# Behind the last product of a streaming encoder layer: 3840 further matmuls of 272 columns

## The chip, the cores and the metric

The kernel runs on one core of a Trainium2 chip. Such a core has a matmul engine (TensorE; PE in the profile, and PEld for its weight loads), a vector engine (VectorE, DVE), a scalar engine (ScalarE, ACT), a general engine (GpSimd, POOL) and an engine that mostly issues transfers (SyncE, SP). A matmul reads a stationary operand, up to 128x128 numbers that a weight load puts into the array, and a moving operand, of which up to 512 columns stream past it; both lie in the on-chip memory SBUF, and the result goes to PSUM, which has eight banks of 512 columns of 32 bits. The metric is the device time of one execution in microseconds (us).

## The reference

One layer of an encoder trunk, for 1024 frames of a new stream and 64 frames of a running one (1088 in all), with a model width of 1024:

```python
def trunk(x, ...):
    m, cs, nk, nv = mixer(rmsnorm(x, g_mix[l]), ...)   # gated convolution and band attention, merged by gates
    x = x + m
    x = x + swiglu(rmsnorm(x, g_ffn[l]), w_ff1[l], w_ff3[l], w_ff2[l])
    return rmsnorm(x, g_final), ...

def swiglu(x, w1, w3, w2):
    return (jax.nn.silu(x @ w1) * (x @ w3)) @ w2
```

The hidden width of the last part is 2816. Outputs are the two normalised results (`y_prompt`, `y_sample`) and the new states of the convolution and the attention. Everything is in float32.

## The kernel before, in words

Each large product is done with split operands. A number is split into a high part, rounded to the type that TensorE takes (`F32R`), and a low part, the rest; a product then is high x high + high x low + low x high, three matmuls that add into one PSUM bank. Above the splitting, large products are cut into 2x2 blocks and done with the seven products of Strassen's scheme, in the order 1, 2, 6, 7, 5, 4, 3 (`STEPS`).

The loop that does this for the input projection and the up and gate products is `run`. For each of the seven products and each of four slices of the depth it issues six matmuls of 272 columns (`HN`): high weights with the high part of the activations, high weights with the low part, low weights with the high part, each for two halves `j` of the frames, which go to two banks. The weights are the stationary operand, and the two halves follow each other with the same weights:

```python
for k in range(4):
    for n, (w, l) in enumerate(((hi, 0), (hi, 1), (lo, 0))):
        for j in range(2):
            mm(t[:, j, :HN], w[:, k, :], x[p][:, l, k, j * HN : (j + 1) * HN], ...)   # L238
```

Other products of 272 columns are plain ones (`product`, L300 to L302): the same three matmuls, one after the other into a single bank.

The last stage is the down product of the feed-forward part (L1508). Its moving operands, 512 columns of the split weights `w_ff2`, lie in rings, one long tile of 4352 numbers per partition for each of the seven products; `ring_of(p)` gives the ring of product `p`. Its stationary operands are tiles `ht` of the hidden activations, read back from `h_d` through SP's queue. The results go to PSUM tiles A (two buffers) and B or D (four buffers in common) of the pool `psD`; ScalarE or VectorE adds them to the accumulators in SBUF (L1518, L1520), and at the end `half_ended` forms the sums of squares (L1448; ScalarE writes the squares, unread, to columns 3072 to 3583 of the first ring), the factor of the normalisation and the output, which leaves by SP's queue (L1459) and ScalarE's (L1457).

The order of the work on each engine is the order in which the program issues it. Tile pools put in the waits that buffers and data need. The program ends with a barrier of all engines (L1587): SP first waits for the counts of all transfers and of the other engines, TensorE's among the last ones.

Of the kernel before, what the change touches and what calls it, by code (L numbers as in the profile page):

```python
# [8 lines left out]
F32 = mybir.dt.float32  # L9
# [6 lines left out]
P = 128  # L16
# [17 lines left out]
HN = HT // 2  # L34
# [30 lines left out]
def encoder_kernel(ctx: ExitStack, tc: tile.TileContext, ins, outs):  # L65
# [1396 lines left out]
    for b, ks in enumerate(blocks):  # L1462
        first, final = b == 0, b == len(blocks) - 1
        nk = blocks[b + 1] if not final else []
        for g in range(2):
# [28 lines left out]
            for si, js in turns:  # L1494
# [47 lines left out]
                if final and g == 0 and si == 4:  # L1542
# [9 lines left out]
                    vec.scalar_tensor_tensor(row, row, r[:TS], gfb[:TS], op0=ALU.mult, op1=ALU.mult)  # L1552
                    nc.sync.dma_start(outs["y_sample"], row)

_OUTS = [
    ("y_prompt", (1024, 1024), (1, 1024, 1024)),
    ("y_sample", (64, 1024), (1, 64, 1024)),
# [33 lines left out]
```

## Time and profile before

| | |
|---|---|
| Median of 2 runs | 1516.43 us (1516.06 to 1516.81) |
| Span of the profiled execution, first to last instruction | 1513.8 us |
| Its own time, with what lies around the span | not in the page; the median is 2.6 us above the span |
| Matmuls, with as many weight loads | 10,178 |
| TensorE busy | 1476.9 us, 98% of the span |
| VectorE, ScalarE, GpSimd busy | 981.2, 682.7, 128.7 us |
| Moved by DMA | 264.73 MB, mean 175 GB/s |
| Mean granted clock of TensorE | 0.994 |

The profile is of one execution. A row that starts with a line number (L238) tells of that line of the kernel; "Da<-mg,wha" means that the tile Da was written from the tiles mg and wha, moving operand first for a matmul; "x4" counts instructions. "128*128" ahead of the shapes is the stationary operand. In the timeline a row begins with its start and its length in us. In the table of stretches each engine has its busy time in us and, in brackets, its instructions in that stretch. Matmuls overlap each other, so that the length of one is longer than the time from its start to the start of the next. SPq and ACTq are the queues on which SP and ScalarE issue transfers, PEq is TensorE's own queue of instructions.

### The profile page before, as it was taken

What the parts mean: (1) busy time and instruction counts of PE and PEld (TensorE: products, weight loads), DVE (VectorE), ACT (ScalarE), POOL (GpSimd) and SP (SyncE); (2) the same over time, 40 slices, a digit from 0 to 9 for tenths busy, and PEclk for the clock granted to TensorE, in tenths of its full rate; (3) what the DMA queues carried; (4) which work ended last, traced back from release to release, by engine and by line L of the source; (5) the groups of instructions that cost most, each with busy time, mean ns of one, the idle gap of its engine ahead of it and who ended that gap; (6) DMA issues with size and microseconds to landing.
All of it is one profiled execution on the core that took longest, in us unless ns stands there. A gap on an engine that the chain in (4) does not pass through costs nothing.

```text
span 1513.8 us, 26451 instructions
## 1 busy us (share of the span) xinstructions
PE 1476.9 (98%) x10178; PEld 1381.1 (91%) x10178; DVE 981.2 (65%) x1843; ACT 682.7 (45%) x1397; POOL 128.7 (9%) x236
## 2 busy tenths in 40 slices
PE   7999999999999999999999999999999999999997
PEld 5799999999999999998889999999999998788886
DVE  6886465642776752763489667666666668857576
ACT  6654433333776752542256444444444445402123
POOL 1210010001111121000100011100001011000000
PEclk9999999999999999999999999999999999999999
DMA  7597524168676529554432434443334449667675
GB/s 233 181 305 245 184 78 135 57 187 234 181 186 176 151 82 293 164 167 145 140 126 77 143 134 152 144 148 120 117 142 157 143 177 317 234 221 235 222 259 202
DMA packets 167518, 264.73 MB, mean 175 GB/s; under 512 B 19008, under 2 KB 103168, under 8 KB 167264
## 3 DMA queue, kind: packets, MB, share of 16 engines
q1 hardware_dynamic: 146736, 198.23, 42.2%
q0 software_dynamic: 19504, 62.71, 11.4%
q10 hardware_dynamic: 1152, 2.10, 0.4%
q8 instruction: 80, 1.31, 0.4%
q14 instruction: 46, 0.38, 0.1%
HBM read 171.06 MB, written 91.92 MB: 174 GB/s over the span
## 4 chain that ended last, share of the span: by engine, by line
PE 79%; DMA 8%; DVE 6%; ACT 3%; issue 3%; SPq 1%; POOL 0%; ACTq 0%; POOLq 0%; DVEq 0%
PE Aa L238 9%; PE Ab L238 9%; PE A L1508 7%; PE Da L238 4%; PE Db L238 4%; PE D L1508 3%; PE Bb L238 2%; PE Ba L238 2%; PE B L1508 2%; PE wo L1066 2%; PE wo L1068 2%; PE wo L1067 2%; PE t L903 2%; PE Ak L238 2%; PE g L300 2%
## 5 line engine op out<-in xcount | busy, mean ns | idle before, releaser
L1508 PE MATMUL A<-ring,ht 128*128 128x512 f32 x528 | 126.6, 393 | 3.6 <-ACT acc L1518 1.9
L1508 PEld LDWEIGHTS A<-ring,ht 128*128 128x128 f32 x528 | 98.8, 188 | 27.2 <-ACT acc L1518 3.2
L300 PE MATMUL g<-xn,whp 128*128 128x272 f32 x384 | 113.2, 295 | 0.0
L301 PE MATMUL g<-xn,whp 128*128 128x272 f32 x384 | 112.0, 292 | 0.0
L302 PE MATMUL g<-xn,wlp 128*128 128x272 f32 x384 | 111.6, 291 | 0.0
L121 ACT CAST ring<-w2r 128x512 fp32r<-128x512 f32 (+1 forms) x78 | 43.4, 587 | 105.7 <-PE A L1508 52.6
L121 ACT CAST hq<-sa 128x512 fp32r<-128x512 f32 x77 | 47.7, 619 | 86.4 <-DVE sa L1239 56.6
L814 DVE CUSTOM_DVE_ANT_0 p<-s,bb 128x640 f32<-128x640 f32 (+5 forms) x72 | 47.5, 661 | 45.5 <-DMA bb<-bias_d 28.6
L1227 POOL DMA_DIRECT2D h_d<-hq x77 | 40.9, 532 | 416.5 <-DVE hq L122 242.1
L122 DVE TENSOR_TENSOR hq<-sa,hq 128x512 fp32r<-128x512 f32 x77 | 53.1, 690 | 33.4 <-ACT hq L121 33.3
L300 PEld LDWEIGHTS g<-xn,whp 128*128 128x128 f32 x384 | 72.6, 189 | 1.0
L302 PEld LDWEIGHTS g<-xn,wlp 128*128 128x128 f32 x384 | 72.6, 189 | 0.5
L301 PEld LDWEIGHTS g<-xn,whp 128*128 128x128 f32 x384 | 72.7, 189 | 0.3
L1508 PE MATMUL D<-ring,ht 128*128 128x512 f32 x264 | 63.9, 393 | 1.3 <-ACT acc L1518 1.3
L122 DVE TENSOR_TENSOR wla<-rawa,wha 128x512 fp32r<-128x512 f32 x56 | 38.5, 687 | 40.5 <-ACT wha L121 40.5
L238 PE MATMUL Aa<-tt,wha 128*128 128x272 f32 x352 | 59.1, 289 | 2.5 <-ACT tt L121 2.5
L1508 PEld LDWEIGHTS D<-ring,ht 128*128 128x128 f32 x264 | 49.5, 188 | 13.1 <-ACT acc L1518 1.8
L122 DVE TENSOR_TENSOR ring<-w2r,ring 128x512 fp32r<-128x512 f32 (+1 forms) x78 | 49.0, 647 | 14.4 <-ACT ring L121 14.2
L238 PE MATMUL Ab<-mg,whb 128*128 128x272 f32 x352 | 58.4, 288 | 0.0
L238 PE MATMUL Aa<-mg,wha 128*128 128x272 f32 x352 | 58.3, 288 | 0.0
L238 PE MATMUL Ab<-tt,whb 128*128 128x272 f32 x352 | 58.2, 287 | 0.0
L121 ACT CAST wha<-rawa 128x512 fp32r<-128x512 f32 x56 | 34.8, 621 | 51.3 <-PE Ab L238 35.3
(519 smaller groups left out, 4368.2 us busy)
## 6 DMA issues: line engine op xcount, KB each, us to landing
h_d<-hq POOLq DMA_DIRECT2D x77, 512.0 KB, 3.5
ht<-h_d SPq DMA_DIRECT2D x154, 256.0 KB, 3.7
rawa<-in_w_ff SPq DMA_DIRECT2D x11, 1024.0 KB, 5.9
rawb<-in_w_ff SPq DMA_DIRECT2D x11, 1024.0 KB, 5.4
w2r<-in_w_ff SPq DMA_DIRECT2D x11, 1024.0 KB, 5.8
qd<-q_d SPq DMA_DIRECT2D x32, 272.0 KB, 4.7
rawp<-in_w_in SPq DMA_DIRECT2D x6, 1024.0 KB, 5.9
u_d<-scr SPq DMA_DIRECT2D x8, 544.0 KB, 4.6
```

What stands on the lines that cost most here:

```text
L121: act.copy(hi, src)
L122: vec.tensor_tensor(lo, src, hi.bitcast(F32), op=ALU.subtract)
L238: mm(t[:, j, :HN], w[:, k, :], x[p][:, l, k, j * HN : (j + 1) * HN], start=p in (1, 2, 7) and k == 0 and n == 0, stop=k == 3 and n == 2, s ...
L300: mm(out, a, p, start=k == 0, stop=False)
L301: mm(out, a, q, start=False, stop=False)
L302: mm(out, b, p, start=False, stop=k == kt - 1)
L814: vec.tensor_tensor_reduce(out=s if len(ps.shape) == 2 else s.rearrange("p (a b) -> p a b", a=2), in0=ps, in1=bias if len(ps.shape) == 2 e ...
L903: nc.tensor.transpose(tp[:, i * P : (i + 1) * P], s[:, i * P : (i + 1) * P], ident)
L1066: mm(ps, x(k, 0), wh, start=f, stop=False)
L1067: mm(ps, x(k, 0), wl, start=False, stop=False)
L1227: nc.gpsimd.dma_start(h_d[p, c - 1], hq.rearrange("p i l t -> p (i l t)").bitcast(F32))
L1508: mm(t, ht[k][:, j, x], w[:, l], start=p in (1, 2, 7) and k == 0 and n == 0, stop=k == len(ks) - 1 and n == 2, skip_group_check=p in (6, 5 ...
```

## The change

Behind the loop of the last stage, 3840 matmuls are added. They write two new PSUM tiles, `pr` and `pq`, that nothing reads. The moving operand is a slice of 272 columns of the first ring, the stationary one a slice of 128 columns of the second ring; both rings hold the split weights of the last block at that point. `a` and `b` are the first columns of the two slices. A setting is a pair of a gap `e` and a shift `d`: `d` moves the stationary operand, by 0 to 120 numbers of 4 bytes in steps of 8, and `e` widens the distance between the two halves of the moving operand, 384 numbers, by 0 to 56 in steps of 8. Each setting is done for four places `k` of the stationary operand, 512 numbers apart, with six matmuls each. In the first 128 settings (`JOINT`) the two halves alternate, in the last 32 (`APART`) all three products of one half come first.

```diff
+    pr = psD.tile([P, 512], F32, tag="A", name="pr", bufs=2)
+    pq = psD.tile([P, 512], F32, tag="BD", name="pq", bufs=4)
+    mv, st = ring_of(1), ring_of(2)
+    JOINT = [(0, 0, 0), (0, 0, 1), (0, 1, 0), (0, 1, 1), (1, 0, 0), (1, 0, 1)]
+    APART = [(w, l, j) for j in range(2) for w, l in ((0, 0), (0, 1), (1, 0))]
+    for six, gaps, starts in ((JOINT, range(0, 64, 8), range(0, 128, 8)), (APART, (0, 16), range(0, 128, 8))):
+        for e in gaps:
+            for d in starts:
+                for k in range(4):
+                    for n, (w, l, j) in enumerate(six):
+                        a, b = 128 + 2048 * l + j * (384 + e), 128 + d + 512 * k + 256 * w
+                        mm(
+                            (pr, pq)[j][:, :HN], st[:, b : b + P], mv[:, a : a + HN],
+                            start=k == 0 and n < 6 and (w, l) == (0, 0), stop=k == 3, skip_group_check=True,
+                        )
```

The outputs are computed as before.

## The prediction

> **What bounds the kernel now.** First the page's head and its row of the granted clock: who is busy, and at what clock.
>
> ```profile
> span 1513.8 us, 26451 instructions
> PE 1476.9 (98%) x10178; PEld 1381.1 (91%) x10178; DVE 981.2 (65%) x1843; ACT 682.7 (45%) x1397; POOL 128.7 (9%) x236
> PEclk9999999999999999999999999999999999999999
> ```
>
> TensorE is busy for 98% of the span, at 9 tenths or more of its clock in every slice. Each of its 10,178 matmuls has a weight load of its own (PEld, same count), also where neighbours share the stationary operand. The time between the starts of two matmuls is therefore a property of the pair, load and matmul. The durations of single matmuls don't give it, because matmuls overlap. It has to come from counts in stretches, or from start times.
>
> The second view is the table of busy times in chosen stretches. The two below hold almost nothing but matmuls of 272 columns: the first is the Strassen loop (L238), whose order the change copies, the second the plain products (L300 to L302), in which all matmuls of a group write one bank.
>
> ```profile
> core 0: us, PE busy (x) PEld busy (x) DVE busy (x) ACT busy (x) POOL busy (x), PEclk, DMA share, GB/s
> 850.00:1150.00 300.00, 300.00 (x2404) 299.94 (x2403) 201.61 (x338) 133.09 (x251) 31.08 (x59) 1.00 0.40 144
> 558.89:598.25 39.36, 39.36 (x315) 39.36 (x314) 6.93 (x9) 11.38 (x25) 6.21 (x12) 1.00 0.85 267
> ```
>
> The counts take in matmuls that began before the window. One lasts 288 ns (rows below), so two or three at a time are in flight, and I take off 2.3. Then the first stretch has 300/2401.7 = **124.9 ns** per matmul, the second 39.36/312.7 = 125.9 ns. The first ran beside a VectorE that was busy two thirds of the time, the second beside one busy 18%, and the quieter one is not the faster. The clock is 1.00 in both.
>
> The timeline shows the same from start to start. The first two rows give one round of six matmuls (four with the high half of the weights, two with the low half), the others its durations and loads:
>
> ```profile
> 901.54 0.66 PE L238 MATMUL Da<-mg,wha 128*128 128x272 f32 x4
> 902.03 0.41 PE L238 MATMUL Da<-mg,wla 128*128 128x272 f32 x2
> ...
> 904.54 0.66 PE L238 MATMUL Aa<-mg,wha 128*128 128x272 f32 x4
> L238 PEld LDWEIGHTS Aa<-mg,wha x352: 187/188/191, 796.0 to 1242.9; 128*128 128x128 f32 x176
> L238 PE MATMUL Aa<-mg,wha x352: 283/288/292, 796.2 to 1243.0; 128*128 128x272 f32 x176
> ```
>
> From 901.54 to 904.54 are four rounds: 24 matmuls in 3.00 us, 125.0 ns each. A load takes 188 ns and a matmul 288 ns, and both come every 125 ns, so they overlap each other.
>
> The third view is the timeline at the end of the span.
>
> ```profile
> 1501.60 2.21 PE L1508 MATMUL D<-ring,ht 128*128 128x512 f32 x9
> 1499.92 0.67 DVE L1520 TENSOR_TENSOR acc<-A,acc 128x512 f32<-128x512 f32 x1
> 1501.80 0.69 DVE L1520 TENSOR_TENSOR acc<-A,acc 128x512 f32<-128x512 f32 x1
> 1503.64 2.20 PE L1508 MATMUL A<-ring,ht 128*128 128x512 f32 x9
> 1505.98 0.68 DVE L1520 TENSOR_TENSOR acc<-A,acc 128x512 f32<-128x512 f32 x1
> 1509.76 0.37 ACTq L1457 DMA_DIRECT2D out_y_prompt<-acc  x1
> out_y_prompt<-acc ACTq DMA_DIRECT2D x4, 256.0 KB, 2.6
> SPq L1587 <- PEq L1587: 0.7, 2, 0.5
> ```
>
> TensorE's last matmul ends at 1503.64 + 2.20 = 1505.84. Behind it come the last additions and the normalisation, and the last output, issued at 1509.76 and landing about 2.6 us later, at 1512.4. The span ends at 1513.8. So TensorE idles 8.0 us at the end, and 1.4 us pass between the last landing and the end, 0.7 us of them SP's waits for TensorE in the closing barrier.
>
> **The change, part by part.** *Removed or moved:* nothing. The orders of VectorE, ScalarE, GpSimd and SP stay as they are, no DMA is added, and the new matmuls stand behind TensorE's last product.
>
> *Their start.* The two new result tiles take banks that the last stage used. pr takes the older of the two "A" banks, last read by the L1520 addition at 1499.92, over at 1500.59. pq takes the bank of the first B product of that stage, read earlier still. So I cost the waits at nothing: the cover is the nine matmuls from 1503.64. If the bank were the younger one, the addition at 1505.98 would hold pr until 1506.66, that is 1 us. The stretch of the first ring tile that ScalarE still writes as scratch (columns 3072 to 3583) is not read: the furthest column read is 128 + 2048 + 440 + 272 = 2888. The nine D matmuls start every (1503.64 - 1501.60)/9 = 0.227 us, so the first new matmul starts at 1503.64 + 9 x 0.227 = **1505.68**.
>
> *Their pace.* 128 + 32 settings of 24 matmuls are 3840. The first 3072 stand in exactly the order of L238: two halves of the columns in turn, in two banks, high weights with the high and the low half of the activations, then low weights. The last 768 do all three products of one half and then those of the other, nearest to L300 to L302, whose three products follow each other in one bank. What no row shows is the particular places: a stationary operand moved in steps of 32 bytes against the moving one, with a fixed relation inside a setting. The matmuls of 512 columns (L1508) show how much places can do in this kernel, since their groups differ only in the tiles' places:
>
> ```profile
> 1480.83 4.24 PE L1508 MATMUL B<-ring,ht 128*128 128x512 f32 x18
> 1484.91 4.36 PE L1508 MATMUL A<-ring,ht 128*128 128x512 f32 x18
> 1489.11 4.36 PE L1508 MATMUL D<-ring,ht 128*128 128x512 f32 x18
> ```
>
> B takes (1484.91 - 1480.83)/18 = 226.7 ns, A (1489.11 - 1484.91)/18 = 233.3 ns: 2.9% between places. By columns, B's rate would make 272 columns 226.7 x 272/512 = 120.4 ns, the **low bound**. The **high bound** for a mean is 124.9 x 1.029 = 128.5 ns, places that lie as far above this kernel's mean as A lies above B. The offsets of the 160 settings run evenly through 512 bytes of relative place, so good and bad ones should average; I take 124.9, the mean of the 300 us in the same order.
>
> *Their sum.* 3839 gaps x 0.1249 = 479.5 us, last start 1985.2. The last matmul adds 0.29: 1985.5. The close lies between the 0.7 of the barrier rows and the 1.4 of the whole stretch; SP has then long passed the output waits and stands at TensorE's count near the end of its list, so I take 1.0. Span after: **1986.5**. The page gives the span of the profiled execution and no time around it; the shown median, 1516.43, lies 2.6 above 1513.8, and I add that: 1989.1.
>
> *What is hidden.* The old tail (8.0 us) now runs beside the new matmuls, so of the 480 us of new work about 472 lengthen the run. Were it not covered (output landing behind the new work), 7 us would come on top.
>
> *A rule that speaks against the sum.* In the rows a matmul of 272 columns takes 124.9 ns in a stream, and one of 512 takes 226.7 to 233.3. The Trainium skill, "TensorE: Matmul & The Clock Gate", section "Back-to-back issue gap", gives for the isolated gap, warm, columns/2.4 + 2.5 ns, an estimate of 115.8 ns at 272 columns, and about 131 ns at 512 columns in a stream of loads and matmuls. By the first figure the sum would be 1954, an estimate from that page; the second disagrees with this trace, which shows 226.7 at least. The same page says (Part 2) that loading the next weights takes no read bandwidth from the running matmul, and so that places could not matter; the 2.9% between A and B doesn't settle it, for the two differ in more than one place.
>
> **The rivals.**
>
> *Free places.* Inside a setting the relative place of the two operands is fixed, where L238 shifts it from matmul to matmul. If most settings then run like B, the pace is 120.4 ns: 1505.68 + 462.2 + 0.29 + 1.0 + 2.6 = **1971.8**. For it: B's rate is steady over 18 matmuls. Against: B is one of three groups, and 850 to 1150 mixes many places at one rate. The page's 115.8 ns would be this rival at its limit; no stretch here ran at it, so I put it at 1 in 50 by itself.
>
> *Colliding places.* Some settings hold load and stream on each other all the time. At 128.5 ns the time is 1505.68 + 493.3 + 3.9 = **2002.9**. The far end is a load that no longer overlaps anything: 188 ns each, 1505.68 + 721.7 + 3.9 = 2231. Against it: loads of 188 ns come every 125 ns wherever this kernel runs such matmuls.
>
> *Not slower.* Nothing reads the two result tiles. If the work were dropped before the chip, or only a part of it ran, the time would stay at **1516**. The point from which it decides: TensorE's idle end hides about (8.0 - 1.4)/0.125 = 53 matmuls, and 2% (30.3 us) is passed when some 300 of the 3840 run. Against it: nothing in the kernel makes a matmul depend on a reader, and the program as built lists all 3840 behind the last product.
>
> **How the numbers follow.** The forecast, a mean pace of 122.6 to 126.8 ns (1980 to 1996), gets 0.72. Free places (below 1980): 0.13, of which 0.02 lie under 1971.8. Colliding places (above 1996): 0.13, of which 0.02 are the exposed loads. Work not run: 0.02. The range goes to 1972 and 2003, the two bounds of the pace; outside it I leave about 0.1. A change within 2% is about what a measurement of this kernel can't tell from none; every case but the last is slower by at least 30%, so slower 0.98, same 0.02, faster 0.
>
> **What the profile after would show.** Right: TensorE's matmuls 14,018, a new group of 3840 of 128x272 at L1566 with 283 to 292 ns each, from about 1505.7 to 1985; no wait in front of it; VectorE, ScalarE and DMA empty behind 1512; windows of 24 matmuls near 3.0 us throughout. Free or colliding places would show as windows that differ by setting: 2.9 us or 3.1 and more for 24. Wrong: a granted clock under 1.00 in the new stretch, gaps of TensorE in it (instructions that don't arrive), or weight loads that begin only when the matmul before has ended.

## The result, and the profile after

The changed kernel takes 1987.41 us (median of 1987.01 and 1987.82), the kernel before 1516.43: a ratio of 1.312, with a 95% interval of 1.309 to 1.315. The forecast was 1989, with a range of 1972 to 2003.

From the page of the changed kernel, the head, the busy row, the granted clock, the queue that carries instructions, and the groups of the new line (busy us and mean ns of one, then the engine's idle time ahead of the group):

```profile
span 1985.7 us, 34131 instructions
PE 1955.0 (98%) x14018; PEld 1859.4 (94%) x14018; DVE 981.5 (49%) x1843; ACT 683.1 (34%) x1397; POOL 128.7 (6%) x236
PEclk9999999999999999999999999999999999999999
q8 instruction: 110, 1.80, 0.4%
L1566 PE MATMUL pq<-ring,ring 128*128 128x272 f32 x1920 | 454.3, 288 | 0.0
L1566 PE MATMUL pr<-ring,ring 128*128 128x272 f32 x1920 | 454.3, 288 | 0.0
L1566 PEld LDWEIGHTS pr<-ring,ring 128*128 128x128 f32 x1920 | 345.2, 188 | 0.0
```

All 3840 matmuls run. None waits (idle 0.0), a matmul still lasts 288 ns and a load 188, the clock stays, and VectorE, ScalarE and GpSimd do what they did. The transfers of instructions (q8) rise from 80 packets to 110, and no gap in TensorE's row answers to it.

Where the new work begins and ends, in the timeline of TensorE, and what SP waits for at the end:

```profile
1500.95 2.20 PE L1508 MATMUL A<-ring,ht 128*128 128x512 f32 x9
1502.99 0.28 PE L1566 MATMUL pr<-ring,ring 128*128 128x272 f32 x1
...
1984.22 0.54 PE L1566 MATMUL pq<-ring,ring 128*128 128x272 f32 x3
```

```profile
SPq L1603 <- PE pq L1566: 474.6, 1, 474.6
SPq L1603 <- DMA out_y_prompt<-acc: 2.3, 3, 1.7
SPq L1603 <- PEq L1603: 0.7, 2, 0.5
```

The first added matmul starts 1502.99 - 1500.95 = 2.04 us after the nine last old ones began, 9 x 0.227: no gap. The last ends at 1984.76, and 0.94 us later the span ends. SP, which closes the program, had the last output long behind it and stood 474.6 us at TensorE's count.

The pace, in one stretch of 400 us (columns as before: the stretch, its length, TensorE busy with its count, granted clock, share of DMA, GB/s):

```profile
1550.00:1950.00 400.00, 400.00 (x3192) 1.00 0.00 1
```

With the 2.3 matmuls in flight taken off, 400/3189.7 = 125.4 ns per matmul.

It is not the same in all settings. Two of them, from the first matmul of the setting to the first of the next: e = 0, d = 40, and e = 32, d = 0.

```profile
1518.03 0.29 PE L1566 MATMUL pr<-ring,ring 128*128 128x272 f32 x1
...
1521.07 0.29 PE L1566 MATMUL pr<-ring,ring 128*128 128x272 f32 x1
```

```profile
1695.73 0.28 PE L1566 MATMUL pr<-ring,ring 128*128 128x272 f32 x1
...
1698.69 0.29 PE L1566 MATMUL pr<-ring,ring 128*128 128x272 f32 x1
```

24 matmuls take 3.04 us in the one and 2.96 us in the other. Worked out in this way from the starts in the trace, these are the paces in ns for three rows of settings, d = 0 to 120 in steps of 8:

```
JOINT e = 0    125.3 126.4 123.5 124.8 126.5 126.7 126.5 125.6 | 125.2 125.4 123.6 123.3 126.5 126.7 126.5 125.6
JOINT e = 32   123.2 125.2 125.2 123.3 125.2 124.8 125.7 124.2 | 123.4 125.2 125.2 123.3 125.2 124.8 125.7 124.2
APART e = 0    125.4 126.5 123.5 124.8 126.5 126.7 126.5 125.6 | 125.2 125.4 123.6 123.3 126.5 126.7 126.5 125.6
```

All 160 lie between 123.2 and 126.8. Most repeat after d = 64, which is 256 bytes: 65 of the 80 pairs agree within a tenth of a nanosecond, and the largest difference is 1.5 ns. At e = 0 the order of the six matmuls changes nothing. At e = 16, where the two halves stand at different places against the weights, it moves single settings by up to 1.0 ns (125.8 ns in the JOINT order and 124.8 in the APART order at d = 0). The mean is 125.42 ns in the first 128 settings and in the last 32; the ten rows of 16 settings average 124.6 to 126.1 ns.

### The profile page after: what moved, and what is told of

Same layout as the page of the kernel before. It is cut to its first block, busy times and chain, and to the rows that moved or that the text cites. A ratio compares the mean times of both kernels' runs of the same rounds, so it can differ in the third digit from the quotient of the medians.

```text
span 1985.7 us, 34131 instructions
## 1 busy us (share of the span) xinstructions
PE 1955.0 (98%) x14018; PEld 1859.4 (94%) x14018; DVE 981.5 (49%) x1843; ACT 683.1 (34%) x1397; POOL 128.7 (6%) x236
## 4 chain that ended last, share of the span: by engine, by line
PE 88%; DMA 4%; DVE 3%; issue 3%; ACT 2%; POOL 0%; SPq 0%; ACTq 0%; POOLq 0%; DVEq 0%
PE pq L1566 12%; PE pr L1566 12%; PE Aa L238 7%; PE Ab L238 6%; PE A L1508 6%; PE Da L238 3%; PE Db L238 3%; PE D L1508 3%; PE g L300 2%; PE Bb L238 2%; PE g L301 2%; PE g L302 2%; PE Ba L238 2%; PE B L1508 2%; PE wo L1066 1%
## 5 line engine op out<-in xcount | busy, mean ns | idle before, releaser
L1566 PE MATMUL pq<-ring,ring 128*128 128x272 f32 x1920 | 454.3, 288 | 0.0
L1566 PE MATMUL pr<-ring,ring 128*128 128x272 f32 x1920 | 454.3, 288 | 0.0
L1566 PEld LDWEIGHTS pr<-ring,ring 128*128 128x128 f32 x1920 | 345.2, 188 | 0.0
L1566 PEld LDWEIGHTS pq<-ring,ring 128*128 128x128 f32 x1920 | 345.1, 188 | 0.0
L121 ACT CAST hq<-sa 128x512 fp32r<-128x512 f32 x77 | 47.7, 620 | 86.5 <-DVE sa L1239 56.5
```

The source lines that it names most:

```text
L121: act.copy(hi, src)
L1566: mm((pr, pq)[j][:, :HN], st[:, b : b + P], mv[:, a : a + HN], start=k == 0 and n < 6 and (w, l) == (0, 0), stop=k == 3, skip_group_check= ...
```

## The experiments

Each replaces the added block of the changed kernel, or adds to it, if nothing else is said.

### One setting instead of 160

```diff
-    for six, gaps, starts in (...):
-        for e in gaps:
-            for d in starts:
+    for turn_n in range(160):
+        e, d = 32, 0        # place_low;  place_high: e, d = 0, 40
```

> All 160 settings are replaced by the one that was fastest in the changed kernel (e = 32, d = 0, alternating halves, 123.2 ns per matmul there). If the pace belongs to the places: 123.2 ns throughout, 3839 x 0.1232 = 473.0 us, some 8.5 us under the changed kernel (1979). If the 123.2 belonged to that moment or to the change from setting to setting, the pace is the mean 125.4 again and the time 1987.

> All 160 settings are replaced by the one that was slowest (e = 0, d = 40, 126.7 ns). Places: 3839 x 0.1267 = 486.4 us, 5 us over the changed kernel (1992) and 13.4 us over the kernel with the fastest setting. Moment or change: 1987, and no difference between the two.

Measured: 1981.89 us (1977.26 to 1984.83 in 4 runs) and 1994.72 us (1991.84 to 1996.48), ratios to the kernel before of 1.3075 [1.3053, 1.3098] and 1.3161 [1.3139, 1.3183]. The same 400 us, of the fast setting's kernel and then of the slow one's:

```profile
1550.00:1950.00 400.00, 400.00 (x3245) 1.00 0.00 1
```

```profile
1550.00:1950.00 400.00, 400.00 (x3160) 1.00 0.00 1
```

That is 400/3242.7 = 123.4 ns and 400/3157.7 = 126.7 ns, and from start to start each of the 160 rounds has its kernel's value, 123.3 or 126.7 ns, to 0.1 ns. The medians differ by 12.8 us where 13.4 were expected. So a pace belongs to a setting, not to the moment. The single times sit 3 us above what was expected; the part ahead of the block varies by more than that (its last matmul starts at 1502.8 in the profile of the changed kernel, at 1507.8 in that of the fast setting).

### A fifth of the work

```diff
-    ... in ((JOINT, range(0, 64, 8), range(0, 128, 8)), (APART, (0, 16), range(0, 128, 8))):
+    ... in ((APART, (0, 16), range(0, 128, 8)),):
```

> Only the last 32 settings are left, 768 matmuls. If each added matmul costs the same from the first on (125.4 ns) and the old tail of 8.0 us is hidden under them: 768 x 0.1254 = 96.3 us minus the 7 us of the tail, 89.3 us over the kernel before, 1605.7. If a fixed cost (a wait ahead of the first, instructions that arrive late) is in the 471 us, the rest per matmul is smaller, and this time lies above or below by that.

Measured: 1602.39 us (1600.98 to 1609.07), 1.0583 times the kernel before [1.0559, 1.0606] (1515.87 there): 86.5 us more, where 89.3 were expected. The block of its profiled run (1609.07 us):

```profile
1510.00:1605.00 95.00, 95.00 (x760) 1.00 0.03 12
```

95/757.7 = 125.4 ns. From this kernel to the whole change, (1987.41 - 1602.39)/3072 = 125.3 ns per matmul. The work is additive, with no fixed cost of its own beyond the few us by which runs differ.

### Other engines busy beside it

```diff
+    da, dc = (rpool.tile([P, 2, D], F32, tag="raw", name=f"beside{i}") for i in range(2))
+    nc.sync.dma_start(da, ...)
+    for i in range(640):
+        vec.tensor_tensor(da[:, 0, :512], da[:, 0, 512:], da[:, 1, :512], op=ALU.add)
+        act.copy(da[:, 1, 512:], da[:, 1, :512])
+        if i % 8 == 0:
+            nc.sync.dma_start(dc[:, i // 8 % 2], ins["w_ff2"][0][:P])
```

> The changed kernel, and beside the added matmuls 640 additions of 128x512 on VectorE, 640 copies of 128x512 on ScalarE and 80 transfers of 512 KB into SBUF. If other engines' traffic in SBUF is part of the pace, the mean over the 160 settings rises from 125.4 by 1 ns or more (4 us); if only the matmul's own two streams set it, it stays within 0.2 ns and each setting keeps its value.

Measured: 1990.68 us, one run. Here the columns after TensorE are its loads, VectorE, ScalarE and GpSimd:

```profile
1550.00:1950.00 400.00, 400.00 (x3192) 400.00 (x3191) 381.23 (x552) 352.40 (x567) 0.00 (x0) 1.00 0.24 74
```

VectorE is busy for 95% of the stretch, ScalarE for 88%, and TensorE does the same 3192 matmuls. Setting by setting the largest difference to the changed kernel is 0.04 ns. Neither the arithmetic of VectorE and ScalarE in SBUF nor these transfers are part of the pace; GpSimd was idle here, so nothing is shown for it. That also answers a rival that the prediction doesn't price, a quiet machine: with everything else idle the pace is no better. The Trainium skill, "SBUF — State Buffer", section "SBUF: two separate sides", says that TensorE, ScalarE and VectorE's own pair of ports never wait for anyone, and that a transfer can't be slowed by an engine's work, nor an engine by a transfer. For TensorE this run agrees, with 0.04 ns at most. (The order on VectorE was not simply the order in which the program issues the work, as the text on the kernel has it: the first two added additions start at 1493.81, ahead of old ones such as L1520 at 1501.94.)

### Which relation of the places

```diff
+    FAMILIES = [
+        [(0, d, d) for d in range(0, 128, 8)],   # both shifted
+        [(0, d, 0) for d in range(0, 128, 8)],   # moving operand alone
+        [(0, 0, d) for d in range(0, 128, 8)],   # stationary alone
+        [(0, 0, d) for d in range(16)],          # stationary, steps of 4 bytes
+        [(e, 0, 0) for e in range(16)],          # gap, steps of 4 bytes
+    ]
...
+        a, b = 128 + c + 2048 * l + j * (384 + e), 128 + d + 512 * k + 256 * w
```

> The 160 settings are replaced by five families, each with alternating halves. First, both operands shifted together by 0 to 480 bytes: flat at the 125.3 of d = 0 if only the distance of the two operands decides, spread like the first row of the changed kernel (123.3 to 126.7) if a place by itself does. Second, the moving operand shifted alone: by distance, the same values as for the stationary operand shifted the other way (126.4, 123.5, 124.8 ... read backwards). Third, the stationary operand shifted alone, as in the changed kernel, a control: the same 16 values within 0.1. Fourth and fifth, shifts of the stationary operand and of the gap by 0 to 60 bytes in steps of 4: if pieces of 32 bytes or more are what collides, plateaus of eight equal values.

Measured: 1747.85 us, one run. The five families, 384 matmuls each, from the table of stretches (the last one ends with the start of its last matmul, so it has 383 gaps):

```profile
1503.83:1551.95 48.12, 48.12 (x386) 1.00 0.07 26
1551.95:1600.15 48.20, 48.20 (x386) 1.00 0.00 1
1600.15:1648.29 48.14, 48.14 (x387) 1.00 0.00 1
1648.29:1696.40 48.11, 48.11 (x386) 1.00 0.00 1
1696.40:1744.50 48.10, 48.10 (x385) 1.00 0.00 1
```

All five average 125.3 to 125.6 ns. Within them, in ns:

```
both shifted      125.3 125.5 125.4 125.1 125.4 125.1 125.5 125.4 125.2 125.4 125.1 125.5 125.4 125.1 125.4 125.1
moving alone      125.5 126.0 126.7 125.3 126.8 125.0 123.5 126.2 125.5 125.5 126.6 126.8 126.6 123.6 123.4 125.5
stationary alone  125.4 125.4 123.5 123.2 126.5 126.7 126.5 125.6 125.2 125.4 123.6 123.2 126.5 126.7 126.5 125.6
by 4 bytes        125.2 125.3 125.9 126.2 125.0 125.8 124.2 124.7 126.5 125.6 126.5 125.5 124.5 125.4 123.4 125.0
gap by 4 bytes    125.1 129.3 126.8 124.9 126.4 127.4 126.5 123.5 124.4 126.7 124.5 123.3 124.7 126.8 125.0 124.0
```

Shifted together, at the one distance that was tried, the operands keep one value within 0.4 ns; shifted apart, they spread over 3.5. So it is mainly the distance between the two that decides, and not a place by itself. The second half of the second row is the third row read backwards within 0.4 ns, as distance demands; its first half is so in part only, with three values off by 0.8 to 1.8 ns. In the third row two values (d = 8 and 24) differ from the changed kernel's by 1.0 and 1.6 ns, although the block is the same. A setting thus can run at more than one pace. What came before it may choose, which is a guess: no run followed it, and distance alone is not the whole account. The plateaus of 32 bytes did not appear: steps of 4 bytes move the pace as much, up to 129.3 ns.

### Narrower loads, other widths

```diff
+    for wide, cols in ((272, 128), (272, 64), (272, 32), (256, 128), (384, 128), (512, 128), (512, 32)):
...
+        mm((pr, pq)[j][:cols, :wide], st[:, b : b + cols], mv[:, a : a + wide], ...)
```

> The 160 settings are replaced by seven groups of 384 matmuls with e = 0 and the 16 shifts d: moving columns x stationary columns 272x128, 272x64, 272x32, 256x128, 384x128, 512x128, 512x32. If the weight load takes read time from the stream, the pace falls with a narrower load, from 125.4 toward 113 to 118 ns at 32 columns, and 512 columns from 231 to some 215. If the pace is a rate per column (0.46 ns as in the kernel before), the load doesn't matter: 125, 125, 125, 117, 176, 231, 231.

Measured: 1946.15 us, one run. The seven groups in this order (TensorE, its loads, VectorE, ScalarE, GpSimd):

```profile
1508.24:1556.43 48.19, 48.19 (x385) 48.19 (x384) 3.43 (x11) 2.61 (x8) 0.00 (x0) 1.00 0.07 26
1556.43:1604.33 47.90, 47.90 (x387) 47.88 (x385) 0.00 (x0) 0.00 (x0) 0.00 (x0) 1.00 0.00 1
1604.33:1651.91 47.58, 47.58 (x386) 41.43 (x384) 0.00 (x0) 0.00 (x0) 0.00 (x0) 1.00 0.00 1
1651.91:1697.38 45.47, 45.47 (x387) 45.47 (x385) 0.00 (x0) 0.00 (x0) 0.00 (x0) 1.00 0.00 1
1697.38:1764.49 67.11, 67.11 (x386) 67.11 (x385) 0.00 (x0) 0.00 (x0) 0.00 (x0) 1.00 0.00 1
1764.49:1853.63 89.14, 89.14 (x385) 72.05 (x385) 0.00 (x0) 0.00 (x0) 0.00 (x0) 1.00 0.00 1
1853.63:1942.70 89.07, 89.07 (x385) 41.50 (x383) 0.00 (x0) 0.00 (x0) 0.00 (x0) 1.00 0.00 1
```

Divided by 384 (383 gaps in the last stretch, which ends with the start of its last matmul): 125.5, 124.7 and 123.9 ns with loads of 128, 64 and 32 columns; 118.4, 174.8 and 232.1 ns for 256, 384 and 512 columns; 232.6 for 512 columns with the narrow load. A load of a quarter of the width takes off 1.6 ns at 272 columns and nothing at 512. The theory that the load steals the stream's time falls, but for that 1.6. Per column the pace is 0.453 to 0.463 ns, most at the least width: a rate of the stream and a small part that does not grow with it. From 256 to 512 columns 113.7 ns come on top, 0.444 ns per column; the line through both leaves 4.7 ns per matmul and gives 125.5 at 272 columns, as measured. This split is an estimate from means over 16 shifts.

### 16-bit operands

```diff
+    mh, sh = (rpool.tile([P, 4096], BF, tag="raw", name=f"half{i}") for i in range(2))
+    for c in range(0, 3072, 512):
+        act.copy(mh[:, c : c + 512], mv[:, c : c + 512].bitcast(F32))
...
+        mm((pr, pq)[j][:, :HN], sh[:, b : b + P], mh[:, a : a + HN], ...)   # 3072 matmuls
```

> Both operands of the added matmuls are turned to 16 bits first (a few us ahead of the first matmul); 3072 matmuls of 272 columns. If the reading of 4 bytes a column is what holds the stream above the bare column rate, the pace falls from 125.4 to 113 to 117 ns and stops depending on the place; if it is a rate of TensorE by columns, 125 stays.

Measured: 1864.77 us, one run. The middle of the block (TensorE's columns alone), and the duration of a load and a matmul (least, median, most, in ns):

```profile
1550.00:1850.00 300.00, 300.00 (x2592) 1.00 0.00 1
L1571 PEld LDWEIGHTS <-half x3072: 96/98/100, 1505.7 to 1861.3; 128*128 128x128 bf16 x192
L1571 PE MATMUL pr<-half,half x1536: 278/279/290, 1505.7 to 1861.3; 128*128 128x272 bf16 x192
```

300/2589.7 = 115.8 ns, and 127 of the 128 rounds of settings have 115.8 to 115.9, whatever the shift (16 shifts in steps of 32 bytes). So the pace fell and stopped depending on the place, as the first of the two expectations has it. The 32-bit type lies 9.6 ns above; both operands were changed here, so this run alone doesn't say which of them costs it. The Trainium skill, "TensorE: Matmul & The Clock Gate", section "Back-to-back issue gap", has a formula for the isolated gap from which an estimate of 115.8 ns for 272 columns is worked out: for 16-bit operands this run agrees, with 115.8 measured.

### Pitch instead of type

```diff
+    for x, y, m, s in ((mh, sh, 1, 1), (mh, sh, 2, 1), (mh, sh, 1, 2), (mh, sh, 2, 2), (mv, st, 1, 1), (mv, st, 2, 1), (mv, st, 1, 2)):
...
+        mm((pr, pq)[j][:, :HN], y[:, b : b + s * P : s], x[:, a : a + m * HN : m], ...)
```

> The 160 settings are replaced by seven groups of 384 matmuls of 272 columns: with operands turned to 16 bits, the moving one, the stationary one, neither or both read with a pitch of 4 bytes (every second number); then the 32-bit type with its usual pitch, and with the moving or the stationary operand read with a pitch of 8 bytes. If the bytes of SBUF that the moving stream passes over set the pace, 16 bits at a pitch of 4 bytes is like 32 bits (125 ns, differing by place), and 32 bits at 8 bytes slower still; if the type sets it, 16 bits stays at 115.8 at either pitch and 32 bits at 125. A pitch of the stationary operand alone should change little (the narrow load, down to a quarter, took off 1.6 ns).

Measured: 1883.42 us, one run. The seven groups in this order, TensorE's columns:

```profile
1508.75:1553.24 44.49, 44.49 (x385) 1.00 0.09 35
1553.24:1599.43 46.19, 46.19 (x386) 1.00 0.01 1
1599.43:1643.91 44.48, 44.48 (x386) 1.00 0.00 1
1643.91:1690.14 46.23, 46.23 (x387) 1.00 0.00 1
1690.14:1738.43 48.29, 48.29 (x387) 1.00 0.00 1
1738.43:1831.62 93.19, 93.19 (x386) 1.00 0.00 1
1831.62:1880.07 48.45, 48.45 (x384) 1.00 0.00 1
```

In ns per matmul: 16 bits 115.9; moving operand at a pitch of 4 bytes 120.3; stationary one 115.8; both 120.4. 32 bits 125.8, or 125.5 without the first of its 16 rounds, in which the type changes; moving operand at a pitch of 8 bytes **242.7**; stationary one 126.5 (383 gaps, as the stretch ends with the last start). So the bytes that the moving stream passes over cost time in both types. The pitch of the stationary operand costs nothing at 16 bits and 1.0 ns at 32; there its shifts are also other places, so that the 1.0 can't be put down to the pitch alone. But 120.3 is neither of the two values expected: about half of the 9.6 ns comes with the pitch, and the pace then differs by place (120.0 to 121.1 ns, where 16 bits without a pitch have 115.8 throughout). The other half comes with the 32-bit type in some further way, which these runs leave open; it has the size of the 4.7 ns that don't grow with the width. The step to 242.7 at 8 bytes fits a stream that reads at most about 9 bytes per ns and partition: 272 x 8/242.7 = 9.0, 272 x 4/120.3 = 9.0, and 4/0.444 = 9.0 from the widths, while the whole pace of the 32-bit type, 125.4, has 8.7. The ceiling is what these numbers suggest, not something that was measured by itself.

### Better places in the kernel before

In the kernel before, with no matmul added:

```diff
+    tpool.tile([P, 8], F32, name="space", tag="space")
     tt = three_sums(tpool, "tt")
```

> The kernel before without any added matmul, with 32 bytes put in front of the tiles of products 6, 7 and 5, so that their rings stand to the stationary operands as those of products 1, 2, 4 and 3 do. Places: the 396 matmuls of 512 columns on these rings fall from 233.4 to 227.2 ns, 2.5 us less, while the Strassen loop's matmuls on the same tiles (1584 in the up and gate products) rise from 124.4 to 125.1, 1.1 us more: 1515.0. If places in the real kernel don't matter: 1516.4.

In the timeline, three of the groups of 18 that the prediction shows (the line is L1509 here):

```profile
1482.29 4.24 PE L1509 MATMUL B<-ring,ht 128*128 128x512 f32 x18
1486.37 4.24 PE L1509 MATMUL A<-ring,ht 128*128 128x512 f32 x18
1490.45 4.24 PE L1509 MATMUL D<-ring,ht 128*128 128x512 f32 x18
```

B, A and D now begin 4.08 us apart from start to start, 226.7 ns per matmul, where A took 233.3 before. Over the whole trace the gaps on the three moved rings fall from 233.4 to 226.8 ns (some 390 gaps), and those of the Strassen loop on the same tiles rise from 124.5 to 125.3. Both went as expected. The time is 1515.41 us against 1515.87 (12 and 17 runs), a ratio of 0.9995 [0.9982, 1.0008]: an expected gain of 1.4 us that single runs, which spread over 1512 to 1523 us here, can't show. It is no version to call better.

## Why the prediction was right

*The start* was set at 1505.68 and was 1502.99. The reasons held (no wait, no gap); the old work ended 2.7 us earlier in this execution, which is within what runs differ by. *The pace* was set at 124.9 ns, from the Strassen loop, and was 125.42: 3839 x 0.5 ns = 2.0 us more. The step behind it, that good and bad places average over 160 settings, held as a step: the settings spread over 123.2 to 126.8, inside the bounds of 120.4 and 128.5, and means over 16 shifts lie closer together, 124.6 to 126.1 by gap. (The family shifted together is no witness to it: it is one distance throughout, whose own pace lies near the mean.) *The close* was 0.94 us, set at 1.0. *The time around the span* was 2.1 us (1987.82 for the profiled execution, 1985.7 of span), set at 2.6. In sum 1502.99 + 481.5 + 0.29 + 0.94 + 2.1 = 1987.8. The 1.6 us between forecast and median are the earlier start and the shorter time around the span (-2.7 and -0.5) against the slower pace (+2.0), with the rest in the close and in the spread of the two runs. So the mechanism held, but part of the nearness is luck: an early start hid a pace that was set too low. The profiled kernels start the block anywhere from 1503.0 to 1509.5, so a miss of several us would have been as good a prediction.

*Free places*: no setting came near 120.4; the best, run alone, held 123.3. The comparison with B of the 512-column products was apt for places (B's place is better, and the moved rings take it over), and the spread from bad to good is alike, 2.9% there and 2.7% between the two single-setting kernels here. What it had wrong is B's rate by columns: 226.7 ns is 0.443 per column, the best place at 272 columns has 0.453, and the widths show that the pace is not in proportion to the columns. *Colliding places*: no setting was above 126.8 in the change; 129.3 exists, at a gap that the change does not have. *Exposed loads*: excluded, a load a quarter as wide changes the pace by 1.6 ns. *Not slower*: all 3840 ran, at full cost from the first on. The 2% that the prediction takes for what a measurement of this kernel can't tell from none is too wide: the runs of the last experiment give a ratio with an interval of 0.26%.

*The rule against the sum*, the estimate of 115.8 ns from the Trainium skill, "TensorE: Matmul & The Clock Gate", section "Back-to-back issue gap", was right for 16-bit operands and wrong for these, which took 125.4. The sentence of that page on loads nearly holds here (a load a quarter as wide takes off 1.6 ns), but that places then could not matter was a step of the prediction's own, and it fails. What it left undecided, whether places matter at all, is decided by the single-setting kernels: they do, by 2.7% between the two.

## What to carry to other kernels

Take the price of a matmul from starts or counts in a stretch of the same shape and type, not from its duration (288 ns here, for 125 from start to start) and not in proportion from another width or type. At 272 columns a matmul with both operands in 32 bits costs 8% more than one in 16 bits (125.4 against 115.8 ns), and a pitch of 8 bytes on the moving operand nearly doubles it, so look at that pitch before the places. The distance between the stationary and the moving operand in SBUF moved the pace of single settings by up to 2.7% in the added work. In the kernel before, moving three rings by 32 bytes made one loop faster and another slower, and the gain in the whole run was not shown. Measure places with many equal matmuls, since in a whole run they drown in the spread.

## What the runs showed of the hardware that I had not expected

- 272 columns of 32 bits at a pitch of 8 bytes take 242.7 ns against 125.8 contiguous; 16-bit ones at a pitch of 4 bytes 120.3 against 115.8. The same pitch on the stationary operand costs nothing at 16 bits and at most 1.0 ns at 32.
- The pace of a setting is steady to 0.1 ns over 160 rounds (shown for two settings), depends mainly on the distance of the operands, for the most part with a period of 256 bytes, and does not change with VectorE 95% and ScalarE 88% busy. A few settings have two paces: at e = 0, d = 24 ran at 124.8 ns in the changed kernel and at 123.2 in the kernel of the families, where d = 88, 256 bytes further on, has 123.2 to 123.3 in both.
- Contiguous 16-bit operands show no dependence on the distance: 115.8 ns at each of 16 shifts in steps of 32 bytes. Finer shifts were not tried.
- For the 32-bit type the pace is not in proportion to the columns: 0.444 ns per further column between 256 and 512 columns, and an estimated 4.7 ns per matmul besides.
